# A two-layer hybrid encoder on one core: end keys first in linear attention, a third tile for the bases of weight sums, and a block's last input pair in two parts

## Chip, cores and metric

The kernel runs on one core of one Trainium2 chip. The metric is the device time of one execution in microseconds (us). A core has five engines with a queue of instructions each: TensorE (PE, with its weight loads shown as PEld), VectorE (DVE), ScalarE (ACT), GpSimd (POOL) and SyncE (SP); DMAs are issued from the queues of SP, ACT and POOL and carried by 16 DMA engines.

## What is computed

The input has 512 tokens of 1024 channels; 16 learned tokens are put in front, so 528 tokens pass through two layers. Each layer is a SwiGLU block, a mixer and a second SwiGLU block:

```python
for l in range(DEPTH):
    h = h + 0.5 * swiglu(rmsnorm(h, norm_gains[l, 0]), ...)
    h = h + mixer(rmsnorm(h, norm_gains[l, 1]), ...)
    h = h + 0.5 * swiglu(rmsnorm(h, norm_gains[l, 2]), ...)
return rmsnorm(h, final_norm)[:, N_META:]
```

The mixer merges two branches. One is softmax attention with 8 query heads and 2 key heads. The other is gated linear attention in both directions, with 4 heads, 64 key channels and 128 value channels, done in chunks:

```python
bcum = jnp.cumsum(log_a, axis=3); btot = bcum[:, :, :, -1:, :]
q_dec = qc * jnp.exp(bcum)
k_inv = kc * jnp.exp(-bcum)
k_end = kc * jnp.exp(btot - bcum)
att = jnp.where(mask, q_dec @ k_inv^T, 0);  o_intra = att @ vc
kv_chunk = k_end^T @ vc          # the state's increment of a chunk
S = exp(btot) * S + kv_chunk;    o_inter = q_dec @ S_prev
```

The "end keys" of the title are `k_end`.

## The kernel before

Activations lie with channels on the 128 partitions and tokens along the free dimension: `h` is 8 chunks of 128 x 528. Every large product is made of three matmuls on values that are split into a high part and a low part (fp32r), high by high, high by low and low by high, with weights as the stationary operand (128x128) and half of the tokens (264, or 256 in the last layer's later part) as the moving one.

**Weights.** All weights pass through `Weights` (L159) in one fixed order, in loads of 128x1024 (512 KB). A load is fetched on SP's queue into one of three raw tiles, then `make` (L225) writes its high part on ACT (`whi`, L238) and its low part on DVE (`wlo`, L239), four tiles of each. Loads are made four ahead and fetched six ahead of use.

**SwiGLU blocks.** The gate and up products are done by a scheme with seven products in place of eight on 2x2 blocks (Strassen-Winograd). For each of 11 pairs of column tiles there are products "1" to "7"; three use blocks of the weights as they are ("1", "2", "4"), and four use sums of blocks, which are made by DMAs that accumulate. In `sums` (L196), when "1" of a pair is made, `s3` is the negative of its block (ACT, L189) plus block 21 (POOL's queue, L194), and `s2` is block 22, loaded on SP's queue into a tile of the pool `wsb` (L184 by way of L203), plus `s3` (L194); they serve "7" and "6". When "2" is made, `s1` is block 21, loaded into a tile of `wsb` (L207), plus block 22 (L194), and `s4` a negative plus `s2`; they serve "5" and "3". So `wsb` holds the bases of two sums of each pair, and it has two tiles. `s3` and `s4` are in the pool `wsa`, with three.

`ffn_steps` (L51) writes the order of the products out by hand. A block that is not the first begins with "1" and "2" of pair 0 together (`two_products`, L566), then "1" and "2" of pair 1, then "6" and "5" of pair 0, then its "7", "4", "3". The sums in PSUM are shared: after "1", "6" and "7" a copy is taken by ACT (`snapshot`, L605 to L608) before the next product accumulates onto the same bank.

**The input of such a block.** For each pair of channel chunks `Norm.pair` (L475) makes seven half-width blocks of the scaled input in a high and a low version; places 0 and 1 (the blocks b11 and b21) serve products "1" and "2", the other five (sums of blocks and the negative of b22) the others. `chunk_of_pair` (L508) calls it after every second chunk of `h` is final, and makes the squares for the RMS norm (`square`, L448). From the sum of squares `rs` (L516) makes the factor that scales the products when they leave PSUM; it is asked for after "6" of pair 0.

**Linear attention.** `gla_pair` (L699) handles two heads, with a pass `d` for each direction. A pass takes the gate's logarithm from PSUM (ACT, L724 to L726; DVE, L727), sums it along tokens (five scans, L731), subtracts the middle of each block (L739, L740) and its total (L741, L742), takes four exponentials on ACT (L746 to L749, or L752 to L755), and multiplies: `qp` on DVE (L757), `kp` on POOL (L758) and the end keys `ke` on DVE (L760). TensorE then transposes `ke` (L764, L765), DVE copies the result out of PSUM (L767, L769), multiplies queries by the state's decay (L777) and copies the decay of each block (L778). From these come the state's increments (L802), the states, and the attention within blocks (L829 and after). Beside it TensorE has projections of the next pair or gates to do (`project`, L685), whose results DVE moves out of PSUM (L527) from two tiles.

**What sets the order.** The program lists instructions; the build gives each engine a fixed queue, by the order in the program and by when it expects operands and tiles to be ready. Instructions in a block marked `tc.high_priority()` go ahead of others that are ready. On the chip, each engine takes its queue in that order and waits where something is not there yet.

Of the kernel before, what the change touches and what calls it, by code (L numbers as in the profile page):

```python
# [10 lines left out]
F32 = mybir.dt.float32  # L11
# [261 lines left out]
def build(tc, ctx, xt, wts, win, par, w2, const, umask, out):  # L273
# [4 lines left out]
    def pool(name, bufs, space=None):  # L278
        if space is None:
            return ctx.enter_context(tc.tile_pool(name=name, bufs=bufs))  # L280
        return ctx.enter_context(tc.tile_pool(name=name, bufs=bufs, space=space))

    one = pool("one", 1)
    slots = {n: pool("s_" + n, b) for n, b in dict(g=16, t=6, rs=2).items()}
    small = pool("small", 4)
    W = Weights(nc, pool("wraw", 3), pool("whi", 4), pool("wlo", 4), wts, win)
    pss = pool("pss", 2, bass.MemoryType.PSUM)
# [18 lines left out]
    def nm(p):  # L306
        count[0] += 1
        return f"{p}{count[0]}"
# [44 lines left out]
    def v2(ap):  # L353
        return ap.rearrange("p (a b) -> p a b", a=2)
# [81 lines left out]
    class Norm:  # L436
# [38 lines left out]
        def pair(self, j):  # L475

            raw = [slot("t"), slot("t")]
            for i, t in enumerate(raw):
                S.activation(t, h(2 * j + i), AF.Identity, scale=col(self.gc + 2 * j + i))
            w = live[0] // 2  # L480
            b11, b12, b21, b22 = [t[:, i : i + w] for t in raw for i in (0, w)]
            begun = j < len(self.x)
            if not begun:
                self.x.append(self.seven())
            hi, lo = self.x[j]

            def parts(at, src):
                S.copy(hi[:, at], src)
                V.tensor_tensor(lo[:, at], src, hi[:, at].bitcast(F32), ALU.subtract)

            if not begun:
                parts(0, b11)
                parts(1, b21)
            S.activation(hi[:, 6], b22, AF.Copy, scale=-1.0)
            V.scalar_tensor_tensor(lo[:, 6], b22, -1.0, hi[:, 6].bitcast(F32), ALU.mult, ALU.subtract)
            t12, t34 = slot("t"), slot("t")
            V.tensor_tensor(t12[:, :w], b12, b11, ALU.subtract)
            V.tensor_tensor(t12[:, w:], b22, t12[:, :w], ALU.subtract)
            parts(slice(2, 4), v2(t12))
            V.tensor_tensor(t34[:, :w], b12, b22, ALU.subtract)  # L500
            V.tensor_tensor(t34[:, w:], b21, t12[:, w:], ALU.subtract)
            parts(slice(4, 6), v2(t34))

        def chunk(self, c):
            self.operand(c)
            self.square(c)

        def chunk_of_pair(self, c):  # L508
            if c % 2 and c < KC - 1:
                self.square(c)  # L510
            if c % 2:
                self.pair(c // 2)
            if c == KC - 1 or c % 2 == 0:
                self.square(c)

        def rs(self, kind="ss"):  # L516

# [22 lines left out]
    def ffn(l, f, norm, done, following):  # L540
# [25 lines left out]
        def two_products(p, names):  # L566

            st = made.setdefault(p, {})
            work = []
            for name, where in zip(names, "XY"):  # L570
                st[where] = pair(p % 2 == 0)
                work.append((st[where][:, :, :w], PLACE[name], *W.op((l, f), p, name)))
            last = len(x) - 1
            for ks in (range(last), [last]):
                for acc, at, hi, lo in work:
                    for k in ks:
                        xh, xl = x[k]
                        for j in range(2):
                            for i, (a, b) in enumerate(((hi, xh), (hi, xl), (lo, xh))):
                                TE.matmul(acc[:, j], a[:, j, k], b[:, at], start=k == 0 and i == 0, stop=k == last and i == 2)  # L580
            for name in names:
                finished(p, name)

# [115 lines left out]
    def gla_pair(l, p, lr, w2t, sr, qa, ka, va, n_out):  # L699
# [14 lines left out]
        def blk(ap):  # L714
            return ap[:, :SEQ].rearrange("p (b t) -> p b t", b=NB)

        for d in range(2):
            z = pair()
            for i, hs in enumerate(halves):
                c0 = p * 256 + d * P  # L720
                TE.matmul(z[:, i, :HF], w2t[:, c0 : c0 + P], lr[:, hs], start=True, stop=True)
            a, g, c, ct_ = slot("t"), slot("t"), slot("t"), slot("t")

            S.activation(v2(a), z[:, :, :HF], AF.Abs)  # L724
            S.activation(a, a, AF.Exp, scale=-1.0)
            S.activation(a, a, AF.Ln, bias=1.0)  # L726
            V.scalar_tensor_tensor(v2(g), z[:, :, :HF], 0.0, v2(a), ALU.min, ALU.subtract)  # L727
            ones = ct[:, C_COS + SEQ : C_COS + SEQ + 1]
            for bs in [b[1] for b in blocks] + [MB]:
                n = bs.stop - bs.start  # L730
                V.tensor_tensor_scan(c[:, bs], ones.broadcast_to([P, n]), g[:, bs], 0.0, ALU.mult, ALU.add)  # L731
            mid = blk(c)[:, :, 63:64].broadcast_to([P, NB, P])
            tot = blk(c)[:, :, 127:128].broadcast_to([P, NB, P])
            mm_, mt_ = c[:, T - 1 : T].broadcast_to([P, META]), None
            src = c
            if d == 1:
                V.tensor_tensor(g, c, g, ALU.subtract)
                src = g
            V.tensor_tensor(blk(a), blk(src), mid, ALU.subtract)  # L739
            V.tensor_tensor(a[:, MB], src[:, MB], mm_, ALU.subtract)  # L740
            V.tensor_tensor(blk(ct_), blk(src), tot, ALU.subtract)  # L741
            V.tensor_copy(ct_[:, MB], a[:, MB])  # L742
            r16 = 1.0 / 16.0
            qp, kp = slot("p"), slot("p")
            if d == 0:
                S.activation(g, a, AF.Exp, scale=-r16)  # L746
                S.activation(a, a, AF.Exp, scale=r16)
                S.activation(c, c, AF.Exp, scale=r16)
                S.activation(ct_, ct_, AF.Exp, scale=-r16)  # L749
                ein, eq, ek, eend = c, a, g, ct_  # L750
            else:
                S.activation(c, a, AF.Exp, scale=-r16)  # L752
                S.activation(a, a, AF.Exp, scale=r16)
                S.activation(ct_, ct_, AF.Exp, scale=-r16)
                S.activation(g, g, AF.Exp, scale=r16)  # L755
                ein, eq, ek, eend = ct_, c, a, g
            V.tensor_tensor(qp[:, :n_out], qa, eq[:, :n_out], ALU.mult)  # L757
            G.tensor_tensor(kp, ka, ek, ALU.mult)  # L758
            ke = slot("p")
            V.tensor_tensor(ke, ka, eend, ALU.mult)  # L760

            tp = pair()
            for b, bs, _ in blocks:
                TE.transpose(tp[:, 0, bs], ke[:, bs], ident)  # L764
            TE.transpose(tp[:META, 1, :P], ke[:, MB], ident)  # L765
            for hh in range(2):
                V.tensor_copy(kt[hh][:, :SEQ].rearrange("p (b k) -> p b k", b=NB)[:, :, d * HD : (d + 1) * HD],  # L767
                              tp[:, 0].rearrange("p (b k) -> p b k", b=NB)[:, :, hh * HD : (hh + 1) * HD])
            V.tensor_copy(ktm[:META, 0:256].rearrange("p (h d k) -> p d h k", d=2, h=2)[:, d],  # L769
                          tp[:META, 1, :P].rearrange("p (h k) -> p h k", h=2))  # L770
            if qin is None:
                qin = [slot("p"), slot("p")]
            e0 = 127 if d == 0 else 0
            for hh in range(2):
                rows = slice(hh * HD, (hh + 1) * HD)
                to = slice(d * HD, (d + 1) * HD)
                V.tensor_tensor(qin[hh][to, :n_out], qa[rows], ein[rows, :n_out], ALU.mult)  # L777
                V.tensor_copy(dec[to, hh, :], blk(ein)[rows, :, e0])  # L778
            prods.append((qp, kp))
# [244 lines left out]
        norm.pools = open_pools("right", **{"x": dict(x=16), "xc": dict(xc=8)}[kind])  # L1024

    def block_pools():
        pools = open_pools("left", wsa=3, wsb=2)
        W.long, W.short = pools["wsa"], pools["wsb"]
        return pools

    def decay_weights(l):

        w, low = slot("t")[:, :512], slot("t")[:, :512]
        wt = one.tile([P, 512], F32R, tag="w2", name=nm("w2"))
        S.dma_start(w, w2[l])
        S.copy(wt, w)
        V.tensor_tensor(low, w, wt.bitcast(F32), ALU.subtract)
        S.activation(w, wt.bitcast(F32), AF.Copy, scale=ct[:, C_PICK : C_PICK + 1])
        V.scalar_tensor_tensor(wt, low, ct[:, C_PICK + 1 : C_PICK + 2], w, ALU.mult, ALU.add)
        return wt  # L1040
# [21 lines left out]
    def mixer(l, norm, done, following):  # L1062

        x, n_out = norm.x, T if l < DEPTH - 1 else SEQ
        pools = open_pools("left", e=8, i=5, p=7, q=6, k=5, lr=1)
        banks = open_pools("left", psum=("mm", "sm"), mm=2, sm=2)
        w2t = decay_weights(l)
        rp = [product("w_in", Acc(k, n_out), x, KC) for k in ("ss", "sm", "mm")]
# [207 lines left out]
```

## Time and profile before

| | |
|---|---|
| median of 3 runs | 2267.22 us (2266.92 to 2269.97) |
| the profiled execution | 2263.49 us |
| its span, first to last instruction | 2261.6 us |
| instructions | 39885 |
| mean granted TensorE clock | 0.992 |
| VectorE busy | 1527.2 us |
| ScalarE busy | 1218.3 us |
| GpSimd busy | 164.7 us |
| read from HBM | 263.07 MB, 117 GB/s over the span |

The profile comes from one execution. Times of the timeline are microseconds from the span's start. In a row of the timeline the columns are start, length, engine, line, operation, the tiles written and read with their shapes, and a count; in brackets stands how long the engine was idle before it and what ended that. A wait for several things is put down to the one that came last. Matmuls are pipelined, so TensorE's busy share says how seldom it stands still, not how near it is to its peak. The first layer's linear attention lies at 422 to 522 us, the second's at 1565 to 1656 us; the SwiGLU blocks after the first begin at about 789, 1148 and 1900 us.

### The profile page before, as it was taken

The page shows a single profiled execution, that of the slowest core. Times are in us where ns is not written, and L with a number is a line of the kernel's source. Part 1 is how long each engine was busy: PE and PEld are TensorE (multiplying, and loading weights), DVE is VectorE, ACT ScalarE, POOL GpSimd, SP SyncE. Part 2 cuts the span into 40 slices and gives each one's busy share as a digit, 9 for nine tenths or more (in the row PEclk, how much of TensorE's full clock was granted, in tenths as well). Part 3 has the DMA queues.
Part 4 walks back from the last instruction along what each step waited for, and adds up shares of the span by engine and source line. Part 5 has one row for each costly group of instructions (what it writes and reads, how often), then busy time and mean ns, then how long its engine had stood idle before and what let it go on. Part 6 is the DMA issues. An engine that isn't in the chain of part 4 may idle for free. (4 is left out here: it accounts for less than half of the span.)

```text
span 2261.6 us, 39885 instructions
## 1 busy us (share of the span) xinstructions
PE 2204.5 (97%) x16538; PEld 2102.9 (93%) x16538; DVE 1527.2 (68%) x2397; ACT 1218.3 (54%) x1824; POOL 164.7 (7%) x184
## 2 busy tenths in 40 slices
PE   8999999999999999999979999999999999999998
PEld 8999999989999999999979999998888888989897
DVE  7657567577876666565676565575789767756565
ACT  8536355344784564453565363454557836636354
POOL 1011000000000010101011010100000000101010
PEclk9999999999999999999999999999999999999999
DMA  8778463211113485867658585732121135869661
GB/s 239 188 177 212 134 168 108 75 57 57 48 38 113 124 203 154 197 174 173 180 139 207 139 217 149 178 105 87 56 68 54 47 121 152 215 155 225 156 181 66
DMA packets 87542, 312.85 MB, mean 138 GB/s; under 512 B 9664, under 2 KB 11840, under 8 KB 87360
## 3 DMA queue, kind: packets, MB, share of 16 engines
q1 hardware_dynamic: 60816, 217.67, 28.6%
q0 software_dynamic: 24768, 90.19, 22.5%
q8 instruction: 130, 2.13, 0.4%
q10 hardware_dynamic: 1776, 2.43, 0.3%
q14 instruction: 52, 0.43, 0.1%
HBM read 263.07 MB, written 2.10 MB: 117 GB/s over the span
## 5 line engine op out<-in xcount | busy, mean ns | idle before, releaser
L597 PE MATMUL ss<-xc,whi 128*128 128x264 f32 (+1 forms) x4720 | 865.1, 285 | 16.9 <-ACT whi L238 9.5
L597 PEld LDWEIGHTS ss<-xc,whi 128*128 128x128 f32 x4720 | 734.7, 189 | 19.7 <-ACT whi L238 10.3
L597 PE MATMUL ss<-xc,wlo 128*128 128x264 f32 (+1 forms) x2360 | 671.4, 285 | 5.1 <-DVE wlo L239 5.1
L404 PE MATMUL ss<-g,whi 128*128 128x264 f32 (+1 forms) x2620 | 482.8, 300 | 0.0
L597 PEld LDWEIGHTS ss<-xc,wlo 128*128 128x128 f32 x2360 | 446.8, 189 | 6.4 <-DVE wlo L239 6.3
L404 PEld LDWEIGHTS ss<-g,whi 128*128 128x128 f32 x2620 | 380.6, 188 | 15.7
L404 PE MATMUL mm<-x,whi 128*128 128x264 f32 (+1 forms) x1712 | 385.8, 315 | 0.0
L238 ACT CAST whi<-w 128x1024 fp32r<-128x1024 f32 (+1 forms) x220 | 230.0, 1046 | 266.2 <-PE ss L404 116.1
L239 DVE TENSOR_TENSOR wlo<-w,whi 128x1024 fp32r<-128x1024 f32 (+1 forms) x220 | 266.6, 1218 | 116.1 <-ACT whi L238 114.8
L238 ACT CAST whi<-raw 128x1024 fp32r<-128x1024 f32 x190 | 199.2, 1048 | 260.2 <-PE ss L597 89.8
L239 DVE TENSOR_TENSOR wlo<-raw,whi 128x1024 fp32r<-128x1024 f32 x190 | 232.1, 1222 | 105.8 <-ACT whi L238 104.8
L404 PE MATMUL ss<-g,wlo 128*128 128x264 f32 (+1 forms) x1310 | 302.2, 300 | 0.0
L404 PEld LDWEIGHTS mm<-x,whi 128*128 128x128 f32 x1712 | 281.2, 190 | 15.3 <-DVE x L393 0.2
L404 PE MATMUL mm<-x,wlo 128*128 128x264 f32 (+1 forms) x856 | 265.2, 314 | 0.0
L404 PEld LDWEIGHTS ss<-g,wlo 128*128 128x128 f32 x1310 | 209.2, 188 | 8.3
L239 DVE TENSOR_TENSOR wlo<-s,whi 128x1024 fp32r<-128x1024 f32 x86 | 105.1, 1222 | 95.7 <-ACT whi L238 95.6
L238 ACT CAST whi<-s 128x1024 fp32r<-128x1024 f32 x86 | 90.3, 1050 | 146.9 <-PE ss L597 128.3
L404 PEld LDWEIGHTS mm<-x,wlo 128*128 128x128 f32 x856 | 161.2, 190 | 7.6
L527 DVE SCALAR_TENSOR_TENSOR t<-ss,rs 128x528 f32<-128x528 f32 (+1 forms) x93 | 64.6, 700 | 126.4 <-PE ss L404 126.3
L189 ACT ACTIVATE s<-w 128x1024 f32<-128x1024 f32 x86 | 91.2, 1060 | 81.7 <-DMA w<-win 46.5
L194 POOL DMA_DIRECT2D w<-win x43 | 37.8, 880 | 599.3 <-DVE wlo L239 222.3
L393 DVE TENSOR_TENSOR g<-c,g 128x528 fp32r<-128x528 f32 (+1 forms) x88 | 61.5, 699 | 22.6 <-ACT g L392 22.6
(280 smaller groups left out, 2829.6 us busy)
## 6 DMA issues: line engine op xcount, KB each, us to landing
w<-win SPq DMA_DIRECT2D x218, 512.0 KB, 4.7
raw<-wts SPq DMA_DIRECT2D x190, 512.0 KB, 3.3
w<-win POOLq DMA_DIRECT2D x43, 512.0 KB, 6.8
s<-win POOLq DMA_DIRECT2D x43, 512.0 KB, 6.7
w<-s POOLq DMA_DIRECT2D x43, 512.0 KB, 5.9
s<-w POOLq DMA_DIRECT2D x43, 512.0 KB, 7.0
h<-xt SPq DMA_DIRECT2D x3, 528.0 KB, 7.6
out<-h SPq DMA_DIRECT2D x2, 512.0 KB, 2.9
```

Of the source, the lines that this page charges most:

```text
L189: self.nc.scalar.activation(t, w, AF.Copy, scale=-1.0)
L194: self.nc.gpsimd.dma_start(t, src, accum_op=ALU.add)
L238: nc.scalar.copy(hi[:, cs], w[:, cs])
L239: nc.vector.tensor_tensor(lo[:, cs], w[:, cs], hi[:, cs].bitcast(F32), ALU.subtract)
L393: V.tensor_tensor(lo, src, hi.bitcast(F32), ALU.subtract)
L404: TE.matmul(acc.half[i][:width], lhs, rhs[:, acc.spans[i]], start=first, stop=last)
L527: V.scalar_tensor_tensor(cut(dst[rows]), pv[rows], -0.5 * f, cut(rs[rows]), ALU.mult, ALU.mult)
L597: TE.matmul(acc[:, j], a[:, j, k], b[:, at], start=bool(begin and k == 0 and i == 0), stop=k == len(x) - 1 and i == 2, skip_group_check=no ...
```

## The change

It has three parts.

- **End keys first.** In each pass of `gla_pair`, what `ke` needs (for `d == 0` the subtraction of the block's total and one exponential; for `d == 1` the exponential of a difference that was already there) and the product itself come directly after the scans, in a block of high priority; the exponential is written to the tile of `ke`. The transposes come next in the program, and only then the subtraction of the middle, the other exponentials, `qp` and `kp`. `kp` is made on DVE instead of POOL.
- **Three tiles for the bases.** `wsb` has three tiles instead of two. To make room, the pool of `rs` has one tile instead of two, and the decay weights (`w2`, 128x512) live in a pool of the mixer instead of one for the whole kernel.
- **The last pair in two parts.** For the last pair of chunks, `early` makes only places 0 and 1 directly from `h`; `late`, called in `two_products` after the matmuls of "1" and "2", makes the other five and the squares of the last two chunks. For all pairs the negative of b22 is made last instead of first.

```diff
-    slots = {n: pool("s_" + n, b) for n, b in dict(g=16, t=6, rs=2).items()}
+    slots = {n: pool("s_" + n, b) for n, b in dict(g=16, t=6, rs=1).items()}
...
             if not begun:
                 parts(0, b11)
                 parts(1, b21)
-            S.activation(hi[:, 6], b22, AF.Copy, scale=-1.0)
-            V.scalar_tensor_tensor(lo[:, 6], b22, -1.0, hi[:, 6].bitcast(F32), ALU.mult, ALU.subtract)
...
             parts(slice(4, 6), v2(t34))
+            S.activation(hi[:, 6], b22, AF.Copy, scale=-1.0)
+            V.scalar_tensor_tensor(lo[:, 6], b22, -1.0, hi[:, 6].bitcast(F32), ALU.mult, ALU.subtract)
...
+        def early(self, j):
+
+            hs = slice(0, live[0] // 2)
+            hi, lo = self.seven()
+            self.x.append((hi, lo))
+            for r in range(2):
+                S.activation(hi[:, r], h(2 * j + r, hs), AF.Identity, scale=col(self.gc + 2 * j + r))
+                V.scalar_tensor_tensor(lo[:, r], h(2 * j + r, hs), col(self.gc + 2 * j + r), hi[:, r].bitcast(F32),
+                                       ALU.mult, ALU.subtract)
+
+        def late(self):
+            self.pair(KC // 2 - 1)
+            for c in (KC - 2, KC - 1):
+                self.square(c)
+
         def chunk_of_pair(self, c):
-            if c % 2 and c < KC - 1:
+            if c < KC - 2:
                 self.square(c)
-            if c % 2:
+            if c == KC - 1:
+                self.early(c // 2)
+            elif c % 2:
                 self.pair(c // 2)
-            if c == KC - 1 or c % 2 == 0:
-                self.square(c)
...
                                 TE.matmul(acc[:, j], a[:, j, k], b[:, at], start=k == 0 and i == 0, stop=k == last and i == 2)
+            norm.late()
             for name in names:
                 finished(p, name)
...
-            mm_, mt_ = c[:, T - 1 : T].broadcast_to([P, META]), None
+            last = c[:, T - 1 : T].broadcast_to([P, META])
+            r16 = 1.0 / 16.0
+            ke = slot("p")
             src = c
-            if d == 1:
-                V.tensor_tensor(g, c, g, ALU.subtract)
-                src = g
+            with tc.high_priority():
+                if d == 0:
+                    V.tensor_tensor(blk(ct_), blk(c), tot, ALU.subtract)
+                    V.tensor_tensor(ct_[:, MB], c[:, MB], last, ALU.subtract)
+                    S.activation(ke, ct_, AF.Exp, scale=-r16)
+                else:
+                    V.tensor_tensor(g, c, g, ALU.subtract)
+                    S.activation(ke, g, AF.Exp, scale=r16)
+                    src = g
+                V.tensor_tensor(ke, ka, ke, ALU.mult)
+            tp = pair()
+            for b, bs, _ in blocks:
+                TE.transpose(tp[:, 0, bs], ke[:, bs], ident)
+            TE.transpose(tp[:META, 1, :P], ke[:, MB], ident)
             V.tensor_tensor(blk(a), blk(src), mid, ALU.subtract)
-            V.tensor_tensor(a[:, MB], src[:, MB], mm_, ALU.subtract)
-            V.tensor_tensor(blk(ct_), blk(src), tot, ALU.subtract)
-            V.tensor_copy(ct_[:, MB], a[:, MB])
-            r16 = 1.0 / 16.0
+            V.tensor_tensor(a[:, MB], src[:, MB], last, ALU.subtract)
             qp, kp = slot("p"), slot("p")
             if d == 0:
                 S.activation(g, a, AF.Exp, scale=-r16)
                 S.activation(a, a, AF.Exp, scale=r16)
                 S.activation(c, c, AF.Exp, scale=r16)
-                S.activation(ct_, ct_, AF.Exp, scale=-r16)
-                ein, eq, ek, eend = c, a, g, ct_
+                ein, eq, ek = c, a, g
             else:
+                V.tensor_tensor(blk(ct_), blk(src), tot, ALU.subtract)
+                V.tensor_copy(ct_[:, MB], a[:, MB])
                 S.activation(c, a, AF.Exp, scale=-r16)
                 S.activation(a, a, AF.Exp, scale=r16)
                 S.activation(ct_, ct_, AF.Exp, scale=-r16)
-                S.activation(g, g, AF.Exp, scale=r16)
-                ein, eq, ek, eend = ct_, c, a, g
+                ein, eq, ek = ct_, c, a
             V.tensor_tensor(qp[:, :n_out], qa, eq[:, :n_out], ALU.mult)
-            G.tensor_tensor(kp, ka, ek, ALU.mult)
-            ke = slot("p")
-            V.tensor_tensor(ke, ka, eend, ALU.mult)
-
-            tp = pair()
-            for b, bs, _ in blocks:
-                TE.transpose(tp[:, 0, bs], ke[:, bs], ident)
-            TE.transpose(tp[:META, 1, :P], ke[:, MB], ident)
+            V.tensor_tensor(kp, ka, ek, ALU.mult)
...
-        pools = open_pools("left", wsa=3, wsb=2)
+        pools = open_pools("left", wsa=3, wsb=3)
...
-        wt = one.tile([P, 512], F32R, tag="w2", name=nm("w2"))
+        wt = slots["w2"].tile([P, 512], F32R, tag="w2", name=nm("w2"))
...
-        pools = open_pools("left", e=8, i=5, p=7, q=6, k=5, lr=1)
+        pools = open_pools("left", e=8, i=5, p=7, q=6, k=5, lr=1, w2=1)
```

## What the change should do to the time

> **What bounds the kernel now.** I read the page first, then TensorE's own waits, then a table of stretches with the granted clock, then the timeline of each engine around the three places that the diff touches.
>
> ```profile
> PE 2204.5 (97%) x16538; PEld 2102.9 (93%) x16538; DVE 1527.2 (68%) x2397; ACT 1218.3 (54%) x1824; POOL 164.7 (7%) x184
> ```
>
> TensorE (PE) is busy for 97% of the span, so only the remaining 57 us and stretches at a low clock can be won; the change removes no matmul. In the next view each row is: who waited, for whom, us in total, times, longest.
>
> ```profile
> PE ss L764 <- DVE p L760: 12.5, 8, 2.1
> PE ss L597 <- ACT whi L238: 9.5, 4, 4.7
> ...
> PE ss L597 <- ACT snap L608: 7.4, 4, 3.8
> PE ss L597 <- DVE wlo L239: 5.1, 6, 2.2
> ```
>
> The largest is the wait of the transposes of the end keys (L764) for their product (L760): eight times, once for each layer, head pair and direction. The L597 rows are weights that come late, nearly all at block starts. The table below (start:end, length, busy us and count of each engine, then the clock) shows what such waits do afterwards.
>
> ```profile
> 454.90:458.20 3.30, 3.30 (x16) 3.06 (x16) 2.71 (x7) 0.00 (x0) 0.00 (x0) 0.55 0.47 146
> 492.40:495.70 3.30, 3.04 (x15) 2.99 (x16) 3.09 (x7) 1.32 (x3) 0.00 (x0) 0.56 0.00 1
> 813.30:816.60 3.30, 3.25 (x14) 2.95 (x15) 1.26 (x2) 1.54 (x2) 0.00 (x0) 0.55 1.03 182
> 1183.30:1188.70 5.40, 5.35 (x24) 5.35 (x25) 2.27 (x3) 0.50 (x1) 0.00 (x0) 0.50 1.01 281
> 1189.00:1194.40 5.40, 5.40 (x46) 5.40 (x45) 3.51 (x6) 4.47 (x5) 1.75 (x2) 0.99 0.63 114
> ```
>
> At full clock 46 matmuls take 5.40 us, 0.117 us each; at half, 24 take as long. A stretch therefore loses its length less 0.117 us a matmul: 1.4 and 1.5 us in the first two rows, which follow waits at L764, 1.7 in the third and 2.6 in the fourth, which follow waits at block starts.
>
> **Part one: end keys first.** The change takes POOL's product kp (L758) to VectorE (DVE) and makes ke and its transposes before the other exponentials. This is one of the eight passes, from the end of the scans on, with the last pass's stretched row at the end.
>
> ```profile
> 433.94 0.69 DVE L739 TENSOR_TENSOR t<-t 128x512 f32<-128x512 f32 x1
> 435.88 2.19 POOL L758 TENSOR_TENSOR p<-i,t 128x528 f32<-128x528 f32 x1 [122.50 <-ACT t L746]
> 436.77 0.63 ACT L749 ACTIVATE t<-t 128x528 f32<-128x528 f32 x1
> 436.79 1.30 DVE L778 COPY dec<-t 64x4 f32<-64x4 f32 x1
> L778 DVE COPY dec<-t x16: 148/166/1302, 436.8 to 1643.2; 64x4 f32<-64x4 f32 x16
> 438.30 0.71 DVE L757 TENSOR_TENSOR p<-i,t 128x528 f32<-128x528 f32 x1
> 438.93 0.70 DVE L760 TENSOR_TENSOR p<-i,t 128x528 f32<-128x528 f32 x1
> 439.77 0.30 PE L764 MATMUL ss<-const,p 128*128 128x128 f32 x1 [1.46 <-DVE p L760]
> 1641.08 1.34 DVE L760 TENSOR_TENSOR p<-i,t 128x528 f32<-128x528 f32 x1
> ```
>
> While POOL runs its 2.19 us, a DVE copy of 64x4 takes 1.30 us where its median is 0.17, and is done just as POOL is. In each pass one DVE instruction is stretched like this, before ke or ke itself; from this one (about 1.1 us over) to the last (1.34 against 0.70) the eight sum to 8.2 us. With POOL's product gone, this goes. DVE pays 0.70 us for kp in its place, as for L757, but behind ke; that puts nothing on TensorE's path as long as projections fill TensorE, and 8 x 0.70 = 5.6 us less 8.2 us leaves DVE with less than before.
>
> The second gain is the chain. From 433.94 to the end of ke (439.63) pass 5.7 us; the new order needs in between a subtraction (0.69 and a small one), one exponential (0.63) and the product (0.70), some 2.2 us, up to 3.5 us less. This does not come off TensorE one for one. Engine queues are fixed at build, and TensorE's is not the program's order, so the build puts instructions where it expects them ready.
>
> ```profile
> 1148.44 0.29 PE L597 MATMUL ss<-xc,whi 128*128 128x264 f32 x1
> 1155.95 0.36 PE L580 MATMUL ss<-xc,whi 128*128 128x264 f32 x1 [0.26 <-DVE t L527]
> ```
>
> Here products of the second weight pair (L597) run ahead of those of the first (L580), which the program writes first. So the transposes will move up with ke, and what TensorE loses is only how much later ke is than the build expects. Of the 12.5 us, 8.2 are the stretched instructions; the other 4.3 (0.54 a pass) is an error that should shrink with the chain, to say 0.37 a pass or 3.0 us. Idle time: 12.5 - 3.0 = 9.5 us, between 5 (only part of the stretching was on the path) and 12.5. The two low-clock stretches should go with their waits: 2.9 us if all their matmuls were full size; some are 128 wide, and I take 2.5. Part one: -12.0 us, between -5 and -15.5.
>
> Where a wait moves: ke's product on DVE now waits at the head of the queue for an exponential of 0.63 us, and behind it stand evacuations of projections (L527), with two PSUM tiles between them and TensorE. One tile is filled by 24 matmuls, 24 x 0.117 = 2.8 us, which covers it. Were that cover gone, it would cost up to 0.63 us a pass, 5 us.
>
> [...]
>
> **Part two: a third tile for the bases of the sums.** At a block start, sums six and five of pair 0 hold both tiles; the bases for pair 1 wait for them. The start at 1148 us:
>
> ```profile
> 1165.35 1.23 DVE L239 TENSOR_TENSOR wlo<-w,whi 128x1024 fp32r<-128x1024 f32 x1 [0.23 <-ACT whi L238]
> 1168.36 4.24 DMA w<-win
> 1173.27 8.90 DMA w<-win
> 1178.14 0.39 PE L597 MATMUL ss<-xc,whi 128*128 128x264 f32 x1 [2.23 <-ACT whi L238]
> 1182.26 1.04 ACT L238 CAST whi<-w 128x1024 fp32r<-128x1024 f32 x1 [4.16 <-DMA w<-win]
> 1183.21 0.59 ACT L608 COPY snap<-ss 128x528 f32<-128x528 f32 x1
> 1183.35 0.59 PE L597 MATMUL ss<-xc,whi 128*128 128x264 f32 x1 [4.70 <-ACT whi L238]
> 1148.00:1166.00 18.00, 13.43 (x102) 12.62 (x102) 16.93 (x33) 12.81 (x23) 0.00 (x0) 1.00 0.09 30
> 1166.00:1183.00 17.00, 10.16 (x78) 9.52 (x78) 9.00 (x10) 10.06 (x13) 3.51 (x4) 0.88 0.88 211
> ```
>
> The first tile is read out at 1166.58; only then are pair 1's bases loaded, the second of them at 1168.36 (4.24 us), accumulated onto at 1173.27 (8.90 us), and ScalarE (ACT) stands at its cast, with a snapshot queued behind it that TensorE needs for the next product. The DMA engines, 9% busy up to 1166, are 88% busy after it. With a third tile, pair 1's sum six is made in the empty stretch (its wait, 2.23 us, goes), and the base of sum five takes the tile that is free at 1166.58: 1166.6 + 4.24 = 1170.8, and an accumulation of between 4.24 us (as the plain load) and 8.90. I take 6, since two of about eight transfers have left the busy stretch: landed at 1176.8, cast at 1177.9. TensorE wants it near 1178.14 - 2.23 + 0.3 = 1176.2. So 1.7 of 6.93 us stays (0 to 4.6), and half of the 2.6 us of low clock: -6.5. On SP's queue, only the load that no longer waits moves; the one behind it waits for the tile as before. Elsewhere the same chain holds:
>
> ```profile
> 812.04 0.39 PE L597 MATMUL ss<-xc,whi 128*128 128x264 f32 x1 [0.90 <-ACT whi L238]
> 813.30 0.39 PE L597 MATMUL ss<-xc,wlo 128*128 128x264 f32 x1 [0.75 <-DVE wlo L239]
> 1923.51 0.38 PE L597 MATMUL ss<-xc,whi 128*128 128x256 f32 x1 [1.63 <-ACT whi L238]
> 1924.77 0.38 PE L597 MATMUL ss<-xc,wlo 128*128 128x256 f32 x1 [0.76 <-DVE wlo L239]
> 1927.88 0.39 PE L597 MATMUL ss<-xc,whi 128*128 128x256 f32 x1 [1.56 <-ACT snap L608]
> ```
>
> At 812: 0.90 + 0.75 = 1.65, and 1.0 of the 1.7 us of clock: -2.6. At 1923: 3.95 less 0.7 that may stay: -3.2. Part two: -12.3 us, between -6 and -15.5. One tile fewer for rs costs nothing: the next rs is made from squares of sums that the old rs scaled. The decay weights' own tile likewise.
>
> **Part three: the last input pair in two parts.** Rows one and two are ready sooner; the squares and five other blocks come later. TensorE's waits near it:
>
> ```profile
> 1165.87 0.39 PE L597 MATMUL ss<-xc,whi 128*128 128x264 f32 x1 [1.70 <-ACT snap L608]
> 1901.37 0.39 PE L597 MATMUL ss<-xc,wlo 128*128 128x256 f32 x1 [0.55 <-DVE wlo L239]
> 1175.40 0.71 DVE L434 SCALAR_TENSOR_TENSOR rs<-t,rs 128x528 f32<-128x528 f32 x1
> 1185.21 0.43 DVE L635 SCALAR_TENSOR_TENSOR c<-c,rs 128x264 f32<-128x264 f32 x1
> ```
>
> Instructions are the same in number and size; only their places move. At best 1.70 + 0.55 = 2.25 us go; at worst the snapshot, now behind all of the late part on ACT, costs 1.70 more. I take -0.7, nearer to no change, because in the first row the snapshot waits for ACT's load, which stays. rs comes later by the two squares, but is done 9 us before it is read; the 5 us that part two takes out of that slack leave 4.
>
> Sum: -12.0 - 12.3 - 0.7 = -25.0 us. The profiled execution took 2263.49 us (span 2261.6), 3.7 us under the median of the runs, 2267.22; I take the difference to the median: **2242.2 us**.
>
> **The rivals.** 0.2% of the time, 4.5 us, is about what a measurement of this kernel can tell from no change.
>
> *The clock stays* (0.08): the stretches of part one, and 1.0 us at 812, have other causes, for instance short matmuls. -25.0 + 3.5 = -21.5: 2245.7 us. The rows speak against it, since each stretch follows a wait. [...]
>
> *The waits at L764 stay as they are* (0.16): the transposes move up by as much as ke does, and the stretching was not what made it late. -12.3 - 0.7: 2254.2 us. Against it: the stretched row is ke itself in the last pass.
>
> *Sum five lands late anyway* (0.12): part two gives 3 us, the waits for sum six in the later block starts: -15.7, 2251.5 us. For it: transfers share engines that are 88% busy.
>
> *Both fail* (0.07), so that the change does not do what it says: -0.7 and some part of 3: about 2264 us.
>
> *Slower* (0.07): TensorE's queue moves the transposes up by the full 3.5 us, while on the chip ke gains only the 1.0 us of stretching, as casts of weights and evacuations stand between. The mean wait goes from 1.56 to 1.56 + 3.5 - 1.0 = 4.1 us: +20 us, and eight low-clock stretches of 1.45 us instead of two, +9; with -13.0 from the rest, +16: 2283 us. It decides from a mean wait of about 2.7 us on. Against it: those casts and evacuations stood there before, too, with a lag of 0.54 us.
>
> **How the numbers follow.** The forecast has 0.50, with its own range from 2234 (parts one and two at their ends, -31, and 2 more) to 2250. The range 2234 to 2258 takes in the first three rivals, and leaves out the last two and tails of 0.06. Faster: 0.50 + 0.08 + 0.16 + 0.12 = 0.86; same 0.07; slower 0.07.
>
> **What would show it.** Right: waits at the transposes of 5 us or less in total, no POOL product, no 64x4 copy near 1.3 us, no clock of 0.55 in linear attention; at the start of layer 1 the first accumulation of pair 1's bases before 1166 us, and waits for casts there under 3 us. Wrong in part one: a total wait still near 12; in part two: a wait over 4 us at that start; wrong altogether: a new TensorE wait over 5 us that is not in the second view above.

## The result, and the profile after

The kernel after takes 2241.47 us (median; 2237.71 to 2246.48), the kernel before 2267.07 us on the same chip: a ratio of 0.989, 95% interval 0.9864 to 0.9917. The forecast was 2242.2. The profiled execution of after took 2237.71 us, 25.8 less than that of before; TensorE's gaps of 0.25 us or more, apart from the first, for the kernel's first weights, sum to 18.7 us where they summed to 39.4. So 20.7 us are waits; the other 5 us are the size of what TensorE's busy time lost with the same matmuls (2204.5 to 2198.5 us), which points to the clock (mean granted 0.996, from the 0.992 of before). The page's first line:

```profile
PE 2198.5 (98%) x16538; PEld 2097.8 (94%) x16538; DVE 1520.7 (68%) x2405; ACT 1218.2 (54%) x1824; POOL 150.9 (7%) x176
```

POOL lost 14 us, the eight products. TensorE's waits after (who waited, for whom, us in total, times, longest):

```profile
PE ss L571 <- ACT whi L238: 7.3, 1, 7.3
PE ss L613 <- ACT snap L624: 4.2, 3, 3.6
PE ss L415 <- ACT c L579: 3.6, 1, 3.6
PE ss L613 <- ACT xc L514: 2.9, 1, 2.9
PE ss L766 <- DVE t L769: 2.0, 4, 0.6
...
PE ss L613 <- ACT xc L488: 1.4, 1, 1.4
...
PE ss L766 <- DVE p L763: 1.3, 4, 0.6
```

Lines have moved: the transposes of the end keys (L764 before) are L766, and their 12.5 us are now 2.0 + 1.3 = 3.3. The row for casts at block starts (L597 <- ACT whi, 9.5 us) is gone; L571 is the wait for the kernel's first weights. New are the two rows for `xc`: the input of the block at the start of layer 1.

A table of stretches (start:end, length, busy us and count of each engine, granted clock, DMA share, GB/s), first of after, with both linear attentions, then a stretch at half clock and a later one at the start of layer 1; below it the two attentions before:

```profile
422.00:522.00 100.00, 97.71 (x791) 91.53 (x791) 72.46 (x164) 49.84 (x104) 0.00 (x0) 1.00 0.19 59
1565.00:1656.00 91.00, 89.57 (x570) 75.93 (x569) 72.85 (x158) 48.54 (x97) 0.00 (x0) 1.00 0.18 60
...
1148.10:1151.50 3.40, 3.40 (x16) 3.40 (x17) 3.03 (x8) 2.82 (x6) 0.00 (x0) 0.50 0.00 0
...
1156.70:1173.70 17.00, 16.84 (x136) 16.44 (x135) 13.34 (x16) 13.54 (x17) 2.63 (x3) 1.00 0.86 207
```

```profile
422.00:522.00 100.00, 92.79 (x723) 86.59 (x721) 71.64 (x155) 44.50 (x95) 8.02 (x4) 0.97 0.17 54
1565.00:1656.00 91.00, 85.15 (x579) 74.12 (x578) 70.16 (x150) 44.85 (x90) 6.12 (x4) 1.00 0.19 64
```

Linear attention has no low clock left, and TensorE is busy for 97.7 of the first one's 100 us instead of 92.8. The block at the start of layer 1 comes some 9 us earlier in after, so its stretch from 1156.7 us on answers to the one from 1166 on in the prediction. There TensorE was busy for 10.16 of 17 us beside DMA engines at 88%; now it is busy for 16.84, beside DMA engines at 86%: the transfers are as dense as before and no longer waited for.

The timeline of after, of the pass that answers to the one in the prediction:

```profile
438.81 0.64 ACT L758 ACTIVATE p<-t 128x528 f32<-128x528 f32 x1
...
439.37 1.21 DVE L239 TENSOR_TENSOR wlo<-raw,whi 128x1024 fp32r<-128x1024 f32 x1
...
440.50 0.70 DVE L763 TENSOR_TENSOR p<-i,p 128x528 f32<-128x528 f32 x1
441.12 0.33 DVE L797 COPY dec<-t 64x4 f32<-64x4 f32 x2
441.35 0.63 PE L766 MATMUL ss<-const,p 128*128 128x128 f32 x4 [0.25 <-DVE p L763]
```

The end keys' exponential runs at 438.81 and is done at 439.45; their product could start there but stands behind a weight split of 1.21 us, and the transposes still wait only 0.25 us. The two copies of 64x4 together take 0.33 us.

The same view at the start of layer 1:

```profile
1136.43 0.86 POOL L194 DMA_DIRECT2D w<-s  x1 [9.56 <-DMA s<-win]
...
1156.05 1.22 DVE L239 TENSOR_TENSOR wlo<-w,whi 128x1024 fp32r<-128x1024 f32 x1 [1.79 <-ACT whi L238]
1157.30 2.70 SPq L184 DMA_DIRECT2D w<-win  x2
...
1161.18 0.89 POOL L194 DMA_DIRECT2D w<-win  x1 [23.88 <-DVE wlo L239]
...
1166.80 1.05 ACT L238 CAST whi<-w 128x1024 fp32r<-128x1024 f32 x1 [0.25 <-DMA w<-win]
```

Pair 1's sum six is accumulated at 1136, before the block starts (1170.56 before). The first tile is read out at 1157.3 here, 9.3 us earlier than the 1166.58 of before, and the base of sum five is loaded into it at once (the first of the two loads in the SPq row). The accumulation of sum five is issued at 1161.18, 3.9 us behind that (6.7 before, at 1173.27), and its tile is cast at 1166.80, another 5.6 us later. TensorE waits for neither sum; a wait of 0.16 us for a snapshot, at 1168, is all that is left there.

### The profile page after: what moved, and what is told of

Read it like the earlier page. It is cut to its first block, busy times and chain, and to the rows that moved or that the text cites. A ratio compares the mean times of both kernels' runs of the same rounds, so it can differ in the third digit from the quotient of the medians.

```text
span 2235.8 us, 39846 instructions
## 1 busy us (share of the span) xinstructions
PE 2198.5 (98%) x16538; PEld 2097.8 (94%) x16538; DVE 1520.7 (68%) x2405; ACT 1218.2 (54%) x1824; POOL 150.9 (7%) x176
## 3 DMA queue, kind: packets, MB, share of 16 engines
q8 instruction: 130, 2.13, 0.4%
## 4 chain that ended last, share of the span: by engine, by line
PE 87%; DVE 5%; ACT 4%; DMA 3%; issue 1%; SPq 0%; POOL 0%; DVEq 0%; ACTq 0%; POOLq 0%
PE ss L613 36%; PE ss L404 27%; PE mm L404 13%; PE sm L404 2%; PE sm L995 1%; DVE wlo L239 1%; DMA w<-win 1%; PE ss L595 1%; PE ss L970 1%; ACT whi L238 1%; ACT t L387 1%; DMA w<-s 1%; PE sm L1011 1%; PE ss L971 1%; PE sm L1012 1%
## 5 line engine op out<-in xcount | busy, mean ns | idle before, releaser
L542 DVE SCALAR_TENSOR_TENSOR t<-ss,rs 128x528 f32<-128x528 f32 (+1 forms) x93 | 64.5, 699 | 126.3 <-PE ss L404 126.2
```

What stands on the lines that cost most here:

```text
L542: V.scalar_tensor_tensor(cut(dst[rows]), pv[rows], -0.5 * f, cut(rs[rows]), ALU.mult, ALU.mult)
```

## Experiments

Each ratio is to runs of the kernel before on the same chips; e11 and e12 stand beside what they complete.

**e1: kp on VectorE, nothing else.** On the kernel before:

```diff
-            G.tensor_tensor(kp, ka, ek, ALU.mult)
+            V.tensor_tensor(kp, ka, ek, ALU.mult)
```

> The kernel before with one line changed: the product kp is made on VectorE instead of GpSimd; ke keeps its place. If GpSimd's product, by stretching one VectorE instruction in each pass, is what makes ke late (the prediction's theory), no 64x4 copy stays near 1.3 us, the waits at the transposes fall from 12.5 us to about 4.3, and the two low-clock stretches go: 8 to 11 us less, a ratio of 0.995 to 0.9965. If ke is late only because it stands behind the other exponentials (rival), the waits stay at 11 to 13 us and the time within 0.1%.

Measured: 2252.67 us, ratio 0.9937 (0.992 to 0.9955). Its waits:

```profile
PE ss L764 <- DVE p L760: 4.9, 8, 1.0
```

12.5 us became 4.9, no 64x4 copy takes over 0.17 us, and no stretch of linear attention is at half clock. One instruction on another engine is most of part one: VectorE was late because POOL's product stretched what ran beside it. The ratio lies below the range that was expected, and its interval reaches into it.

**e2: part one alone.** The whole hunk of `gla_pair`, with two base tiles and the last pair in one part.

> Part one alone, on the kernel before. If the three parts act at different places and add up, the waits at the transposes are about 3.5 us as in the changed kernel, the waits for casts at the block starts stay at 9.5 us, and the time falls by 11 to 13 us, a ratio near 0.9947. If moving the transposes ahead pays only because the rest moves too (rival), the waits stay above 6 us and the time falls by under 7 us.

Measured: 2251.49 us, ratio 0.9929 (0.991 to 0.9947).

```profile
PE ss L597 <- ACT whi L238: 8.3, 3, 6.3
...
PE ss L750 <- DVE t L753: 1.9, 4, 0.6
PE ss L750 <- DVE p L747: 1.4, 4, 0.5
```

The transposes (L750 here) wait 3.3 us, 1.6 less than in e1, and the block starts are much as before. The ratio is again lower than expected: 16 us (12 to 20) where 11 to 13 were. The two ratios cannot be told apart, so what the new order adds to e1 is shown by the waits alone.

**e3: part two alone.** `wsb=3`, one tile for `rs`, the decay weights in the mixer.

> Part two alone: three tiles for the bases, with the two pools that make room. If late bases are what ScalarE and TensorE wait for at the block starts, the waits of L597 for casts go from 9.5 us to under 1 and those for the snapshot from 7.4 to about 4 (3.6 of them at the kernel's start); with the low clock the time falls by 12 to 16 us less some 1.6 us that the additional load costs at the kernel's start: a ratio of 0.9935 to 0.9955. If part three is needed for it (rival: the casts wait behind the input's blocks on ScalarE), over 4 us of the waits stay and the ratio is above 0.997.

Measured: 2261.71 us, ratio 0.9977 (0.9961 to 0.9992), less than expected. Its waits:

```profile
PE ss L597 <- ACT snap L608: 14.0, 6, 8.2
...
PE ss L597 <- ACT whi L238: 0.7, 1, 0.7
```

The casts' waits went from 9.5 to 0.7 us as they should; a snapshot's wait of 2.54 us stays at the start of layer 1, and the snapshots' sum doubled, by a wait of 8.2 us from 82 us on: in the kernel's first block, which the prediction had left out. The timeline there, first of before, then of e3:

```profile
46.45 0.88 POOL L194 DMA_DIRECT2D s<-win  x1 [6.30 <-ACT s L189]
49.41 0.87 POOL L194 DMA_DIRECT2D w<-win  x1 [2.08 <-DVE c L635]
...
75.34 0.86 POOL L194 DMA_DIRECT2D w<-s  x1 [7.40 <-DMA w<-win]
76.65 0.87 POOL L194 DMA_DIRECT2D w<-win  x1 [0.45 <-issue]
...
81.71 1.05 ACT L238 CAST whi<-w 128x1024 fp32r<-128x1024 f32 x1 [1.97 <-DMA w<-s]
```

```profile
48.21 0.88 POOL L194 DMA_DIRECT2D w<-win  x1 [7.55 <-DVE rs L434]
48.75 1.23 POOL L194 DMA_DIRECT2D s<-win  x1
...
76.79 0.87 POOL L194 DMA_DIRECT2D w<-win  x1 [7.46 <-DMA w<-win]
77.42 1.14 POOL L194 DMA_DIRECT2D w<-s  x1
...
88.70 1.04 ACT L238 CAST whi<-w 128x1024 fp32r<-128x1024 f32 x1 [9.83 <-DMA w<-s]
...
90.29 0.81 PE L597 MATMUL ss<-xc,whi 128*128 128x264 f32 x2 [8.19 <-ACT snap L608]
```

POOL issues the accumulations one behind the other. With a third tile the build put that of sum five (w<-win) ahead of that of sum six (w<-s), which TensorE needs first. The brackets show it: at 75.34 of before POOL's queue stands 7.40 us for the base of sum six, at 76.79 of e3 it stands 7.46 us for the base of sum five, with sum six behind it. `s<-win` goes out 2.3 us later, `w<-s` 2.1 us later and right behind another accumulation, and it is cast 11.3 us after its issue instead of 6.4. ScalarE stands at that cast for 9.83 us with the snapshot behind it, and TensorE for 8.19.

**e4: part three alone.**

> Part three alone. The prediction takes 0.7 us for it, the two traces about none: the waits at the block starts apart from the sums stay near 6 us, a ratio of 0.999 to 1.0005. Rival: it shortens the chain into the block at its start, so that the waits of 2.24, 1.70 and 0.55 us there go without the other parts, 3 to 5 us less, a ratio of 0.998 to 0.9985.

Measured: 2268.92 us, ratio 1.0008 (0.9994 to 1.0021): nothing. At the start of layer 1 the waits ahead of those for the sums are 0.56, 1.42 and 1.80 us, 3.8 in sum, where before they were 4.8.

**e5: after, with kp back on POOL.**

```diff
-            V.tensor_tensor(kp, ka, ek, ALU.mult)
+            G.tensor_tensor(kp, ka, ek, ALU.mult)
```

> The kernel after with the product kp back on POOL; the end keys keep their place ahead of everything else. Theory: it was POOL's long product, next to the short copies and products of VectorE, that made the transposes of the end keys late; with the end keys first, ke is done before kp begins, so kp can only stretch what comes behind it (the 64x4 copies and the products for the next steps), which does not decide. Then the waits at the transposes of the end keys stay near 3.5 us in sum, and the time is that of the kernel after: ratio to before 0.988 to 0.990. Rival: the stretched copies and products behind it delay the next direction's end keys as before; then the waits rise to 6 to 9 us, half clock comes back to linear attention, and the ratio is 0.991 to 0.993.

Measured: 2248.71 us, ratio 0.9919 (0.9903 to 0.9935). From its waits and its timeline:

```profile
PE ss L766 <- DVE p L763: 4.4, 5, 1.4
...
PE ss L766 <- DVE t L769: 1.7, 3, 0.6
```

```profile
447.17 1.68 POOL L784 TENSOR_TENSOR p<-i,t 128x528 f32<-128x528 f32 x1 [125.16 <-ACT t L772]
...
447.60 1.82 DVE L763 TENSOR_TENSOR p<-i,p 128x528 f32<-128x528 f32 x1
```

My theory fell: the end keys are first in the program, but a weight split held their product until 447.60, and kp, begun at 447.17, stretched it to 1.82 us. The transposes wait 6.1 us, which is the rival's figure, though without its half clock: no single wait exceeds 1.4 us. The ratio says less, since this execution also has a wait of 7.10 us in the first block.

**e6: parts one and two without three.**

> Parts one and two without part three. Part three alone gave 1.0008, parts one and two alone 0.9929 and 0.9977. Theory of parts that add up: 0.9929 times 0.9977 is 0.9906, so 0.990 to 0.9915, and the trace has the wait of several us near 82 us that part two alone showed in the first block (8.19 us), because the third tile's load sits ahead of the sums' loads there. Rival: that wait belongs to one execution, and part two is worth the 8 to 12 us that its block starts show: then the ratio is 0.988 to 0.990, the first 100 us hold no more than 8 us of waits, and part three is worth nothing beside the others either.

Measured: 2244.52 us, ratio 0.9893 (0.9877 to 0.9909). Neither side holds whole: the ratio is the rival's, the trace has the theory's wait, 6.55 us at 84 us. Part three is again worth nothing that can be measured. The product of the two ratios (0.9906) lies inside the interval, so the parts may add up; the interval is too wide to show that they do exactly.

**e7: the ones' cast later.** What bounds after at 60 us is one instruction on ScalarE that waits for the constants:

```diff
     def load_constants():
         S.dma_start(ct, const)
         S.dma_start(mask, umask)
-        S.activation(ones64, b64, AF.Copy, scale=float(HD))
...
         meta = n_out == T
+        if l == 0:
+            S.activation(ones64, b64, AF.Copy, scale=float(HD))
         kt = project(x, rs, "i")
```

> The kernel after with one instruction moved: the cast that makes the ones of the heads, which stands on ScalarE behind the load of the constants at 50 us, is issued at the first attention instead. Theory: the 3.60 us that TensorE waits at 59.9 us are that cast holding up ScalarE's queue until the constants have landed; without it the wait goes, and of the 6.8 us at half clock behind it 3.4 go too: 3.6 plus 1.7, ratio 0.9865 to 0.988. Rival: the loads of the start are late in any case, and what ScalarE held back meets the next late load within 30 us: the sum of the waits of the first 100 us stays at 7 to 8 us, ratio 0.988 to 0.990.

Measured: 2237.51 us, ratio 0.9864 (0.9848 to 0.988). The wait at 60 us and the half clock behind it are gone; 0.75 us at 67 and 1.80 us at 82 came up. The waits of the first 100 us, apart from that for the first weights, are 5.6 us where after has 7.7.

**e8: early for two pairs.** At the start of layer 1, VectorE makes pair 2's sums and differences (L499 is one of them) before it takes chunk 6 out of PSUM (L542), and ScalarE stands idle behind that until it can make the blocks of pair 3 (L514). The timeline of after:

```profile
1143.12 0.90 PE L613 MATMUL ss<-xc,whi 128*128 128x264 f32 x3 [1.43 <-ACT xc L488]
...
1144.80 0.43 DVE L499 TENSOR_TENSOR t<-t,t 128x264 f32<-128x264 f32 x1
1145.49 0.70 DVE L542 SCALAR_TENSOR_TENSOR t<-ss,rs 128x528 f32<-128x528 f32 x1
...
1146.72 0.70 DVE L551 TENSOR_TENSOR h<-h,t 128x528 f32<-128x528 f32 x1
1147.45 0.52 ACT L514 ACTIVATE xc<-h,par 128x264 fp32r<-128x264 f32 x1 [1.56 <-DVE h L551]
...
1148.02 0.52 PE L613 MATMUL ss<-xc,whi 128*128 128x264 f32 x1 [2.90 <-ACT xc L514]
```

```diff
         def late(self):
-            self.pair(KC // 2 - 1)
+            for j in (KC // 2 - 2, KC // 2 - 1):
+                self.pair(j)
...
-            if c == KC - 1:
+            if c in (KC - 3, KC - 1):
                 self.early(c // 2)
```

> The kernel after with part three's cut made for pair 2 as well as pair 3: of both only the two plain blocks are made ahead, and both are finished behind the first two products. Theory: what TensorE waits for at the start near 1141 us (1.43 for a cast of pair 2, 2.90 for the plain blocks of pair 3) is VectorE's queue, which holds pair 2's sums and differences ahead of the last two chunks; without them there both waits go, with the half clock of 3.4 us behind them: 4.3 plus 1.7, ratio 0.9865 to 0.988. Rival: the work is only moved behind the first two products, and the third one waits for it at each of three starts: waits of 1 to 3 us at a new line or place, ratio 0.988 to 0.992.

Measured: 2236.55 us, ratio 0.9865 (0.9849 to 0.988). Waits of 0.56, 1.43 and 2.90 us became 0.87, 1.00 and 0.38, and the half clock at 1148 is gone: 4.9 us are 2.25. The theory held; the rival's waits behind the first products (1.00 and 0.38) are there, but are 1.4 us in sum. The edit also takes pair 2's work off ScalarE's queue at that place, so VectorE's part in the gain rests on the bracket at 1147.45.

**e9: two tiles in the first block, three later**, on after:

```diff
-    def block_pools():
-        pools = open_pools("left", wsa=3, wsb=3)
+    def block_pools(n=3):
+        pools = open_pools("left", wsa=3, wsb=n)
...
-    bp = [block_pools()]
+    bp = [block_pools(2)]
```

> The kernel after with two tiles for the bases in the first block and three in the later ones. Over all traces so far the wait of TensorE between 81 and 87 us was 0, 1.98, 0 and 2.13 us with two tiles and 8.19, 0.48, 7.10, 6.55, 1.80 and 3.69 us with three. Theory: the third tile lets a base's load start some 26 us earlier, in among the loads that the first block waits for, and what the sums then lack lands 0.5 to 8 us late there. With two tiles in that block the wait is 0 to 2.2 us again, the starts of the later blocks stay without waits for the casts, and the time is 2 to 6 us under that of the kernel after: ratio 0.9862 to 0.988. Rival: the wait there is chance (how far the loads of one execution spread), and the tiles have no part in it: then it is between 0 and 8 us here as well, and the ratio is 0.9885 to 0.990.

Measured: 2236.84 us, ratio 0.9865 (0.9845 to 0.9886). From its timeline:

```profile
75.42 0.86 POOL L194 DMA_DIRECT2D w<-s  x1 [7.63 <-DVE c L657]
76.73 0.87 POOL L194 DMA_DIRECT2D w<-win  x1 [0.45 <-DVE wlo L239]
```

POOL's order is that of before again, TensorE does not wait at all between 81 and 90 us, and no cast is waited for at the later block starts. The single tile for `rs` and the moved decay weights are still there, so they are not what costs in the first block.

**e11: the mirror image, before with the third tile in the first block only.** The pools of e3, with `block_pools(3)` for the first block and 2 for the others.

> The kernel before with the third tile in the first block only. The later blocks keep two tiles and so their waits for the casts (9.5 us). Theory: the third tile costs the first block 0.5 to 8 us at 81 to 87 us and up to 3.4 us of halved clock behind it, and wins nothing in that block: ratio 1.001 to 1.004, with a wait of over 2.2 us there. Rival: no price in the first block: ratio 0.999 to 1.001 and a wait of 0 to 2.2 us there.

Measured: 2275.76 us, ratio 1.0035 (1.0022 to 1.0048): 7.8 us slower (5 to 11). From its timeline:

```profile
92.05 1.04 ACT L238 CAST whi<-w 128x1024 fp32r<-128x1024 f32 x1 [6.97 <-DMA w<-s]
...
93.64 0.81 PE L597 MATMUL ss<-xc,whi 128*128 128x264 f32 x2 [4.16 <-ACT snap L608]
```

This execution, the slowest of its twelve, also waits 6.50 us at 39 us, where before has 1.30; why is not shown. With e9 it settles where part two's cost comes from: the third tile in the first block.

**e12: after once more.**

> The kernel after, unchanged, once more, since three edits are weighed against it and its own profile shows a wait of only 0.48 us in the first block, where five other kernels with three tiles there showed 1.80 to 8.19 us. Theory (the third tile's price in the first block differs from execution to execution): a wait of another length between 81 and 88 us, 1 to 8 us, and a ratio of 0.988 to 0.991. Rival (that kernel's own order spares it the wait): 0 to 1 us there again, and 0.987 to 0.989.

Measured: 2242.57 us, ratio 0.9899 (0.9882 to 0.9917), with a wait of 1.90 us at 89 us. Over all traces, the wait that begins between 81 and 90 us is 0, 1.98, 0, 2.13, 0 and 0.87 us with two tiles in the first block (before, e1, e2, e4, e9, e10), and 8.19, 0.48, 7.10, 6.55, 1.80, 3.69, 4.16 and 1.90 with three (e3, after, e5 to e8, e11, e12): means of 0.8 and 4.2 us. Within one kernel it differs from execution to execution (0.48 and 1.90), so one profile does not price it. Nor is it the whole price: TensorE's waits from 21 to 110 us sum to 4.2 to 6.5 us with two tiles and 5.1 to 13.2 with three. POOL's order goes with the tiles. With two, `s<-win` goes out first near 46 us and `w<-s` near 75, in all six traces; with three, `w<-win` goes out ahead of the one in all eight and ahead of the other in all but e7.

**e10: the edits of e7, e8 and e9 together.**

> Three edits on the kernel after together: the ones' cast moved to the first attention (alone 0.9864), pair 3's cut made for pair 2 too (alone 0.9865), two tiles for the bases in the first block. If each gain is its own stretch's (3.6 us and its clock at 60 us, 4.3 us and its clock at 1141 us, 2 to 6 us and their clock at 84 us), they add up: 0.989 less 0.0025, 0.0025 and 0.0015 to 0.0025, so 0.9815 to 0.984. Rival: what moved from 60 us meets the loads at 66 to 84 us, so the first and the last edit share one gain: 0.984 to 0.986.

Measured: 2228.85 us, ratio 0.983 (0.9812 to 0.9847): the gains add up as the theory has it, though the interval just reaches the rival's range (0.984 to 0.986). This is the best version, some 13 us under after. Singly, e7, e8 and e9 lie close to what their intervals can tell from after (0.9864 to 0.9917); together they are clear of it. Its waits:

```profile
PE ss L571 <- ACT whi L238: 7.2, 1, 7.2
PE ss L613 <- DVE wlo L239: 3.0, 5, 0.9
PE ss L766 <- DVE t L769: 1.9, 4, 0.6
PE ss L613 <- ACT snap L624: 1.9, 2, 1.0
PE ss L414 <- ACT c L579: 1.9, 1, 1.9
```

Apart from the first weights, no wait is over 1.9 us.

## Why the prediction came out right

**Part one (-12.0).** Right, by its own steps. The waits fell by 9.2 us (9.5 was the step), 3.3 stayed (3.0), and both low stretches went. From profile to profile e2 is 12.6 us faster; against the median of before it is 16 us (12 to 20), in good part because before's profiled execution (2263.49) lay under its median beside e2 (2268.89). The stretching by POOL was the larger term: e1 alone takes 7.6 of the 9.2 us, where the working gave it 8.2. Against the rival "slower" the prediction says that "those casts and evacuations stood there before, too, with a lag of 0.54 us"; that they cost little held only with kp off POOL, as e5 shows the same queue with kp on POOL at 6.1 us. The feared wait of VectorE's queue for the exponential shows nowhere on TensorE.

**Part two (-12.3).** Right at the later block starts, wrong as a whole. At the start of layer 1 the base of sum five did wait for the tile that comes free first, as the working has it, only 9.3 us earlier in the run. From there to the issue of its accumulation 3.9 us pass (4.24 taken), and 5.6 more to the cast (6 taken). So the starts gained a little more: of the 12.5 us of waits that the working named, 0.2 are left in after, where it took off 10.1. With part two alone 3.2 us of them stay, 2.54 at that start. Against that, the first block was priced at nothing, and there the third tile costs 5 to 11 us (e11). The failed step is the sentence that on the queues only the load moves that no longer waits: it speaks of SP's queue, and on POOL's, which it does not look at, accumulations changed places. So alone part two is worth 5 us (2 to 9), not 12.

**Part three (-0.7).** Not contradicted: e4 and e6 cannot be told from zero, nor from -0.7. The 4.8 us of waits at the start of layer 1 ahead of those for the sums became 4.9 in after, in other places; e8 shows why: what stands in VectorE's queue there, pair 2's sums and differences, sets that start, and not the last pair's seven blocks alone.

**The rivals.** "The waits stay" and "the clock stays" fell with part one's rows; "sum five lands late" with the cast at 1166.80; "slower" with waits that shrank, not grew. The signs named were met: 3.3 us at the transposes, no 64x4 copy over 0.17 us, no low clock in linear attention, the first accumulation for pair 1 at 1136 us, casts' waits of 0. That the sum is right to a microsecond is luck. By e2 part one is worth some 4 us more than its term, by e3 part two some 7 less, each known to some 4 us, and the first block's cost, which is in no term, takes back what the starts gained beyond theirs.

## What to carry to other kernels

Where a short operation takes eight times its median, as a 64x4 copy did here (1.30 us against 0.17), look at which engine ends together with it before reordering its queue. A buffer added to let loads run ahead can also change the order in which a queue issues what works on them; read that order at each place where the pool is used, the cold start above all, and give the buffer only to the stages that want it. Before moving work earlier on a queue, see what it now stands in front of.

## What the runs showed of the hardware

**Where the clock halved.** In all fourteen traces the low stretches are 3.41 us long or a multiple of it (but for the last, which the end of the trace cuts), at a clock of 0.5, and within one execution they start on one grid of 3.41 us. In before, five are 3.41 us long and one 10.24; in after, two are 3.41 us long and one 6.83. I cut TensorE's idle time, worked out from the matmul records, into the cells of that grid. A cell with over 1.8 us idle was followed by a cell at half clock 56 times out of 56. Among cells with under 1.44 us idle, some 9000 were followed by full clock, and 16 by half: ten of these 16 were at half clock already, with 0.7 to 1.3 us idle, and six are a stretch at some 570 to 590 us that six of the traces show, with no wait ahead of it. In between it went both ways (12 half, 24 full). Before and after alone give 7 of 7 over 1.8 us (four and three), 3 half of 1293 under 1.44, and 2 half, 3 full in between. So in these traces about half a cell of idle time went ahead of half clock, in one wait or several; what halves the clock is not shown. In before, 1.83 us at 490.84 were followed by half clock, and so were 0.90 and 0.75 us in one cell, at 812 and 813. At the start of layer 1 of after the 2.90 us were followed by the row at 1148.10, the 1.43 us in the cell ahead of it by full clock. The transposes' waits in after, 0.6 us at the longest, have no half clock behind them (1.00 in both linear attentions); for a wait of 2 us in one cell an estimate is 1.7 us more, half of the 3.41 us at half clock.

**POOL beside VectorE.** A 64x4 copy took 0.17 us (median in before) and up to 1.30 us beside POOL's product; a 128x528 product took 0.70 us, and 1.82 beside it in e5. In before the copy of 1.30 us ended at 438.09 and POOL's product beside it at 438.07; in e5 the product of 1.82 us ended at 449.42, 0.57 us after POOL's. With that product on VectorE no 64x4 copy took over 0.17 us (after), with it back on POOL one took 1.27 (e5); by what means POOL's product held them up is not shown.
